# 14 of the 44 row tiles of a down projection, computed in 2x2 blocks with seven products instead of eight

## The chip, the cores and the metric

One core of a Trainium2 chip runs the whole program. The metric is the device time in microseconds, the median of three runs. Five engines have queues of their own: TensorE (PE, with PEld for its weight loads), VectorE (DVE), ScalarE (ACT), GpSimd (POOL) and SyncE (SP), which here only issues DMAs. Each queue is worked off in order.

## The reference, cut to what matters

One layer of a decoder trunk on 512 tokens with 2048 features. The part that changes is the gated feed-forward at its end:

```python
D_FF = 5632                                    # 44 tiles of 128
a, v = jnp.split(h @ w_up, 2, axis=-1)         # h: (512, 2048), w_up: (2048, 2 * D_FF)
conv = conv_b + sum(conv_w[t] * shifted(a, t) for t in range(3))
x = x + gate2 * ((jax.nn.silu(conv) * v) @ w_down)     # w_down: (D_FF, 2048)
return rms_norm(x, final_norm_g)
```

`gate2` is the last sixth of `silu(c) @ ada_w + ada_b`. All arithmetic has to keep float32 accuracy.

## The kernel before, in words

Features lie on partitions and the 512 tokens along the free dimension. For accuracy each operand of a matmul is split into a rounded high part and a low rest (fp32r, both 4 bytes), and a product is three matmuls: high x high, high x low, low x high (`mm3`, L147 to L149). Splitting takes one ACT instruction (a cast to the high part) and one DVE instruction (the subtraction): L118 and L119 for weights, L174 and L175 for activations.

**Up projection.** The first three of 44 tile pairs (gate and value) are plain matmuls with 512 columns. The other 41 ("groups", numbered from 0) are computed by a Strassen-Winograd scheme (`up_group`, `product`, `Fast`): the weights of a group are cut into 2x2 blocks (two halves of the features, and gate against value), the activations too (two halves of the features, two halves of the tokens), and seven products P1, Q5, P2, P7, Q3, P6, Q4, in this order, take the place of eight. A product ("step") is 8 feature tiles x 3 matmuls with 256 columns (L804 to L806); each product sums into one of four PSUM banks, and a few ACT and DVE instructions (L936 to L948) join them into the gate tile `a` and the value tile `v`.

`Fast` prepares the weights. Per group four DMAs of 512 KB on SP (L763) and two accumulating ones on POOL (L774) load blocks, two DVE additions form sums of blocks (L768 `first`, L778 `fourth`), and each of the seven weight operands is split (L118, L119). The event table puts each of these some steps ahead of its product. The pool `rp` for raw loads has nine buffers (two of them hold `ca`, the activated vector c, until the last modulation tile is done, and the weights of a running and of a coming group hold up to six), the pool `wp` for split weights has three, so the split for a step can begin when the product three steps back is done. The activations of the seven products (`hop`) are made once by `make_h` just ahead of group 0 and inside it: 28 splits of 128x512 and their sums.

At the end of a group the tile pair of the group before goes through `glu` (conv, silu, times v; L720 to L724) and is written to the DRAM tensor `ad` (L1010).

**Down projection.** It goes over the 44 tiles in chunks of `JD` = 10, 10, 10, 10 and 4. For each of 16 output tiles of a chunk, 10 weight tiles make 30 matmuls with 512 columns, and L1048 adds the result, times gate2 (`mods[5]`), to the residual `x1`, which is loaded back from DRAM in chunk 0 (L1019). The activations are read from `ad` two tiles at a time and split (`act_pair`, L989); for the first chunk this is done during the last up group (`drain`). The 16 tiles of gate2 are computed during chunk 0 (`ada_next`): two rows of 512 KB loaded (L94), multiplied with `ca` and summed on DVE (L100, twice a tile), and joined (L109). The last chunk of 4 runs in two halves of 256 tokens, with the final norm.

The order in each queue is not that of the code alone: a scheduler places instructions by its own estimates of when they are ready. The rows of the queues below are what it made.

Of the kernel before, what the change touches and what calls it, by code (L numbers as in the profile page):

```python
# [14 lines left out]
P = 128  # L15
# [6 lines left out]
JD = (10, 10, 10, 10, 4)  # L22
NDS = 16 * 40 // 8
# [13 lines left out]
def trunk_kernel(ctx: ExitStack, tc: tile.TileContext, x, c, ada, w_in, w_qft, pool_w, w_out, w_up, w_dn, cst, msk, out):  # L37
# [66 lines left out]
    def ada_tile(m, k):  # L104
        a = gemv(ada[m * KT + k], ca)
# [498 lines left out]
    adaq += [(m, k) for m in (2, 4, 3, 5) for k in range(KT)]  # L604
# [75 lines left out]
    while len(adaq) > 2 * KT:  # L680
        ada_next()
# [53 lines left out]
    class Fast:  # L735
# [55 lines left out]
    fast = Fast([[w_up[j, q] for q in range(4)] for j in range(NP0, NJ)])  # L791
    nstep = [0]

    def product(n, i, opnd, banks):
# [6 lines left out]
        for k in range(8):  # L801
# [4 lines left out]
            E.matmul(o, wL[:, sl], mH, start=False, stop=k == 7, skip_group_check=True)  # L806
# [80 lines left out]
    ad = dp.tile([NJ, P, T], F32, tag="ad", name="ad", bufs=1)  # L887

    def late(jj):
        for i in (2 * jj, 2 * jj + 1):  # L890
            V.tensor_scalar(raws[i], raws[i], biases[:, KT + i:KT + i + 1], None, ALU.add)
        nc.sync.dma_start(ad[jj], glu(jj, raws[2 * jj], raws[2 * jj + 1]))
# [12 lines left out]
    for jj in range(NP0):  # L905
# [16 lines left out]
    def up_group(n):  # L922
# [3 lines left out]
        for i in SEQ:  # L926
            if n == 0:
                while len(hop[i]) < 8:
                    next(mh, None)
            product(n, i, hop[i], b)  # L930
            if n == NJ - NP0 - 1:
                del hop[i]
                drain(i)
# [66 lines left out]
    def drain(i):  # L1000
        act_more(min(JD[0] // 2, i))
        if i >= P6:
            dn.load(2 * (i - P6) + 2)
            dn.split(i - P6 + 1)

    pend = None
    for n in range(NJ - NP0):
        r = up_group(n)
        if pend is not None:
            nc.sync.dma_start(ad[pend[0]], glu(*pend))  # L1010
        pend = r
    nc.sync.dma_start(ad[pend[0]], glu(*pend))

    x1 += [None] * KT
# [74 lines left out]
def _layout(inputs):  # L1089
# [70 lines left out]
```

## Time and profile before

| | |
|---|---|
| median of three runs | 2088.27 us (2086.49 to 2090.19) |
| profiled execution | 2086.56 us, span 2084.7 us |
| granted TensorE clock, mean | 0.995 |
| PE busy | 2048.5 us (98% of the span), 13010 matmuls |
| DVE busy | 1548.2 us (74%) |
| ACT busy | 925.0 us (44%) |
| DMA moved | 414.64 MB, 199 GB/s over the span |
| up projection in products | from 793 to 1587 us |
| down projection | from 1587 to 2070 us |

A busy PE says little, since matmuls overlap: the mean of one 256-column matmul reads 276 ns, while they start 113 ns apart. What counts is the number that start in a stretch, and the idle time that a wait puts in front of them.

### The profile page before, as it was taken

To read this page: it belongs to the slowest core of one execution; us is meant where nothing else is said; L and a number is where in the kernel's file an instruction comes from. 1 tells how busy PE (TensorE), PEld (TensorE's weight loads), DVE (VectorE), ACT (ScalarE), POOL (GpSimd) and SP (SyncE) were. 2 spreads that over 40 slices of the span, in tenths; PEclk is the share of its full clock that TensorE was granted. 3 is DMA by queue.
4 is the path that set the end of the run, shared out by engine and by line. 5 is a ranking of instruction groups with operands and counts; after the bars stand their busy time and mean duration, and the time that the engine had idled before them with its cause. 6 is when DMAs were issued, how large, how long until landed. Compare 5 with 4: busy or idle time off the path is not lost.

```text
span 2084.7 us, 32504 instructions
## 1 busy us (share of the span) xinstructions
PE 2048.5 (98%) x13010; PEld 1835.3 (88%) x13010; DVE 1548.2 (74%) x2311; ACT 925.0 (44%) x1330; POOL 94.1 (5%) x123
## 2 busy tenths in 40 slices
PE   7999999999999999999999999999999999999997
PEld 6888888888888888999999999999999888888887
DVE  8898899988977688887777777777778754343446
ACT  4323555565733355554544554455454222222234
POOL 0100000000000000000000000000000000000001
PEclk9999999999999999999999999999999999999998
DMA  9886877755586545787777777777778964343402
GB/s 372 314 295 211 280 236 251 247 174 181 192 301 220 195 170 124 205 229 177 179 185 180 173 187 183 177 174 191 182 176 301 323 240 142 102 134 102 139 30 81
DMA packets 127639, 414.64 MB, mean 199 GB/s; under 512 B 13536, under 2 KB 17920, under 8 KB 127488
## 3 DMA queue, kind: packets, MB, share of 16 engines
q1 hardware_dynamic: 115680, 369.57, 52.3%
q0 software_dynamic: 11808, 43.00, 12.5%
q8 instruction: 102, 1.67, 0.3%
q14 instruction: 49, 0.40, 0.1%
HBM read 392.58 MB, written 19.94 MB: 198 GB/s over the span
## 4 chain that ended last, share of the span: by engine, by line
PE 88%; DVE 6%; DMA 2%; issue 2%; ACT 1%; SPq 0%; DVEq 0%; POOL 0%; POOLq 0%; ACTq 0%
PE mm L147 11%; PE mm L149 11%; PE mm L148 11%; PE mm L806 7%; PE mm L804 7%; PE mm L805 7%; PE sm L805 5%; PE sm L806 5%; PE sm L804 5%; PE sm L148 4%; PE sm L147 4%; PE sm L149 4%; DMA raw<-in_dram 2%; DVE raw L100 1%; DVE w L119 1%
## 5 line engine op out<-in xcount | busy, mean ns | idle before, releaser
L118 ACT CAST w<-raw 128x1024 fp32r<-128x1024 f32 x491 | 516.3, 1052 | 766.2 <-PE mm L149 312.3
L119 DVE TENSOR_TENSOR w<-raw,w 128x1024 fp32r<-128x1024 f32 x491 | 600.3, 1223 | 323.4 <-ACT w L118 323.2
L147 PE MATMUL mm<-hh,w 128*128 128x512 f32 x1120 | 437.1, 396 | 14.9 <-ACT w L118 13.1
L149 PE MATMUL mm<-hh,w 128*128 128x512 f32 x1120 | 437.5, 391 | 0.0
L148 PE MATMUL mm<-hl,w 128*128 128x512 f32 x1120 | 436.6, 390 | 0.0
L806 PE MATMUL mm<-hh,w 128*128 128x256 f32 x1312 | 362.6, 276 | 0.7 <-DVE w L119 0.7
L805 PE MATMUL mm<-hl,w 128*128 128x256 f32 x1312 | 362.6, 276 | 0.3 <-DVE hl L175 0.2
L804 PE MATMUL mm<-hh,w 128*128 128x256 f32 x1312 | 362.5, 276 | 0.0
L100 DVE SCALAR_TENSOR_TENSOR raw<-raw,ca 128x1024 f32<-128x1024 f32 x192 | 232.1, 1219 | 74.9 <-DMA raw<-in_dram 74.1
L805 PE MATMUL sm<-hl,w 128*128 128x256 f32 x984 | 273.5, 278 | 4.5 <-DVE hl L175 4.5
L804 PE MATMUL sm<-hh,w 128*128 128x256 f32 x984 | 273.4, 278 | 0.0
L806 PE MATMUL sm<-hh,w 128*128 128x256 f32 x984 | 273.0, 277 | 0.0
L147 PEld LDWEIGHTS mm<-hh,w 128*128 128x128 f32 x1120 | 210.9, 188 | 59.1 <-ACT w L118 13.1
L149 PEld LDWEIGHTS mm<-hh,w 128*128 128x128 f32 x1120 | 210.7, 188 | 45.4 <-DVE w L119 0.8
L148 PEld LDWEIGHTS mm<-hl,w 128*128 128x128 f32 x1120 | 211.0, 188 | 42.6 <-issue 0.5
L806 PEld LDWEIGHTS mm<-hh,w 128*128 128x128 f32 x1312 | 246.3, 188 | 1.3 <-DVE w L119 1.1
L805 PEld LDWEIGHTS mm<-hl,w 128*128 128x128 f32 x1312 | 246.3, 188 | 0.7 <-DVE hl L175 0.7
L804 PEld LDWEIGHTS mm<-hh,w 128*128 128x128 f32 x1312 | 246.3, 188 | 0.4 <-ACT hh L174 0.4
L805 PEld LDWEIGHTS sm<-hl,w 128*128 128x128 f32 x984 | 186.0, 189 | 5.3 <-DVE hl L175 5.3
L804 PEld LDWEIGHTS sm<-hh,w 128*128 128x128 f32 x984 | 185.9, 189 | 0.5 <-ACT hh L174 0.2
L806 PEld LDWEIGHTS sm<-hh,w 128*128 128x128 f32 x984 | 186.1, 189 | 0.1
L148 PE MATMUL sm<-hl,w 128*128 128x512 f32 x384 | 149.4, 389 | 0.0
(198 smaller groups left out, 2532.6 us busy)
## 6 DMA issues: line engine op xcount, KB each, us to landing
raw<-in_dram SPq DMA_DIRECT2D x612, 512.0 KB, 4.8
raw<-in_dram POOLq DMA_DIRECT2D x82, 512.0 KB, 5.4
ad<-t SPq DMA_DIRECT2D x44, 256.0 KB, 3.1
raw<-ad SPq DMA_DIRECT2D x22, 512.0 KB, 3.8
t<-in_dram SPq DMA_DIRECT2D x32, 256.0 KB, 6.0
x1d<-t SPq DMA_DIRECT2D x16, 256.0 KB, 4.1
t<-x1d SPq DMA_DIRECT2D x16, 256.0 KB, 6.0
out_dram<-ob SPq DMA_DIRECT2D x8, 512.0 KB, 3.3
```

What stands on the lines that cost most here:

```text
L100: V.scalar_tensor_tensor(out=r, in0=r, scalar=1.0, in1=vec[i], op0=ALU.mult, op1=ALU.mult, accum_out=a[:, i:i + 1])
L118: A.copy(h, r)
L119: V.tensor_tensor(l, r, h.bitcast(F32), op=ALU.subtract)
L147: E.matmul(o, wH, mH, start=start, stop=False)
L148: E.matmul(o, wH, mL, start=False, stop=False)
L149: E.matmul(o, wL, mH, start=False, stop=stop)
L804: E.matmul(o, wH[:, sl], mH, start=first and k == 0, stop=False, skip_group_check=True)
L805: E.matmul(o, wH[:, sl], mL, start=False, stop=False, skip_group_check=True)
L806: E.matmul(o, wL[:, sl], mH, start=False, stop=k == 7, skip_group_check=True)
```

## The change

The first 14 tiles of the down projection are taken in 2x2 blocks with seven products, by the functions that the up projection has: 7 pairs of row tiles on one axis (even and odd tile), output tiles f and f + 8 on the other, and the two halves of the tokens. That gives 8 further groups (41 to 48) of seven products with 7 tiles x 3 matmuls with 256 columns each. The chunks behind them are `JD` = 10, 10, 6 and 4. In detail:

- `emit`: the results of `glu` for these 14 tiles are not written to `ad`. For each pair four DVE instructions of 128x256 form the sums that the products need, and four DMAs write seven blocks to a DRAM tensor `od`.
- `operands`, `handover`: during the last up group, behind each step, the activations of the same step of the down groups are read from `od` (two DMAs, 512 and 384 KB, in rows of 1 KB) and split: three splits of 128x512 and one of 128x256 per step, on ACT and DVE. Behind the steps of the last down group, the work of the old `drain` is done.
- `Fast` gets 8 more groups, with weight blocks of 128x896.
- The gate2 tiles (`mods[5]`) move from chunk 0 into the up groups 7, 9, ... 37, one in each.
- Both `x1` tiles of a down group are loaded at its head.

```diff
-JD = (10, 10, 10, 10, 4)
-NDS = 16 * 40 // 8
+SD = (7,)
+JD = (10, 10, 6, 4)
+NSP = sum(SD)
+NDS = 16 * sum(JD[:-1]) // 8
...
+        def new(self, n):
+            return rp.tile([P, U], F32, tag="raw", name="raw")[:, :self.groups[n][0].shape[-1]]
...
+    for m in SD:
+        for _ in range(8):
+            groups.append([])
+            for _ in range(4):
+                groups[-1].append(w_ds[off:off + P * m * P].rearrange("(p n) -> p n", p=P))
+                off += P * m * P
+    fast = Fast(groups)
...
-        for k in range(8):
+        for k in range(len(opnd)):
...
+    def emit(j, t):
+        if j >= 2 * NSP:
+            nc.sync.dma_start(ad[j - 2 * NSP], t)
+            return
+        held[j] = t
+        if j ^ 1 not in held:
+            return
+        p = j // 2
+        a, b = held.pop(2 * p), held.pop(2 * p + 1)
+        s, r = tt(), tt()
+        lo, hi = slice(0, 256), slice(256, 512)
+        V.tensor_tensor(s[:, lo], a[:, hi], b[:, hi], op=ALU.subtract)
+        V.tensor_tensor(s[:, hi], a[:, lo], a[:, hi], op=ALU.subtract)
+        V.tensor_tensor(r[:, hi], a[:, lo], s[:, lo], op=ALU.subtract)
+        V.tensor_tensor(r[:, lo], b[:, lo], r[:, hi], op=ALU.subtract)
+        for i, q in ((0, b), (2, s), (4, r)):
+            nc.sync.dma_start(od[i:i + 2, p].rearrange("i p t -> p i t"), q.rearrange("p (i t) -> p i t", i=2))
+        nc.sync.dma_start(od[6, p], a[:, lo])
...
+    def ada_load(k):
+        arow[k] = gemv_load(ada[5 * KT + k])
+
+    for k in range(KT):
+        todo[7 + 2 * k, P1] = partial(ada_load, k)
+        todo[7 + 2 * k, Q4] = partial(ada_tile, 5, k, arow)
...
+    def operands(c, i):
+        p0, m = sum(SD[:c]), SD[c]
+        res = []
+        for q in range(0, m, 4):
+            w = min(4, m - q)
+            r = rp.tile([P, U], F32, tag="raw", name="raw")
+            nc.sync.dma_start(r[:, :w * 256].rearrange("p (m t) -> p m t", m=w),
+                              od[OIX[i], p0 + q:p0 + q + w].rearrange("m p t -> p m t"))
+            for g in range(0, w, 2):
+                src = r[:, g * 256:(g + min(2, w - g)) * 256]
+                if w - g > 1:
+                    res += split2(src)
+                else:
+                    t = tp.tile([P, T], F32R, tag="t", name="hh")
+                    h, l = t[:, :256], t[:, 256:]
+                    A.copy(h, src)
+                    V.tensor_tensor(l, src, h.bitcast(F32), op=ALU.subtract)
+                    res.append((h, l))
+        return res
...
+    for n in range(NJ - NP0):
+        r = (n + NP0,) + group(n, hop, hop_ready if n == 0 else None, handover(0, hop) if n == NJ - NP0 - 1 else None)
+        if pend is not None:
+            emit(pend[0], glu(*pend))
+        pend = r
+    emit(pend[0], glu(*pend))
+    ng = NJ - NP0
+    for c in range(len(SD)):
+        for f in range(8):
+            if c == 0:
+                x1_load(f)
+                x1_load(f + 8)
+            a, v = group(ng, dop[c], None, handover(c + 1, dop[c]) if f == 7 else None)
+            ng += 1
+            for i, q in ((f + 8, v), (f, a)):
+                V.scalar_tensor_tensor(out=x1[i], in0=q, scalar=mods[5][:, i:i + 1], in1=x1[i], op0=ALU.mult, op1=ALU.add)
...
-            if ci == 0:
-                ada_next()
-                x1_load(f + 1)
```

The DVE queue in an up group of before, from the end of `glu` on. The three `w` rows ahead of L778 are the splits for P7, Q3 and P6, the one at the end is that for Q4; L768 and L778 are `first` and `fourth`:

```order
L724 TENSOR_TENSOR t_8480<-t_8480,t_8033 128x512
L119 TENSOR_TENSOR w_8527<-raw_8273,w_8527 128x1024
L768 TENSOR_TENSOR raw_8617<-raw_8500,raw_8498 128x1024
L119 TENSOR_TENSOR w_8555<-raw_8419,w_8555 128x1024
L119 TENSOR_TENSOR w_8583<-raw_8392,w_8583 128x1024
L778 TENSOR_TENSOR raw_8392<-raw_8392,raw_8362 128x1024
L942 TENSOR_TENSOR th_8494<-th_8494,mm_8488 128x256
L119 TENSOR_TENSOR w_8614<-raw_8392,w_8614 128x1024
```

The same stretch in group 9 of the change, one of the 16 groups with a gate2 tile:

```order
L726 TENSOR_TENSOR t_8971<-t_8971,t_8516 128x512
L102 SCALAR_TENSOR_TENSOR raw_9017,acc_9199<-raw_9017,ca_86 128x1024
L121 TENSOR_TENSOR w_9021<-raw_8764,w_9021 128x1024
L121 TENSOR_TENSOR w_9049<-raw_8910,w_9049 128x1024
L102 SCALAR_TENSOR_TENSOR raw_9018,acc_9199<-raw_9018,ca_87 128x1024
L773 TENSOR_TENSOR raw_9111<-raw_8990,raw_8988 128x1024
L121 TENSOR_TENSOR w_9077<-raw_8883,w_9077 128x1024
L983 TENSOR_TENSOR th_8984<-th_8984,mm_8978 128x256
L783 TENSOR_TENSOR raw_8883<-raw_8883,raw_8853 128x1024
L111 SCALAR_TENSOR_TENSOR mod5_102<-acc_9199,cs_78 128x1
L121 TENSOR_TENSOR w_9108<-raw_8883,w_9108 128x1024
```

The two L102 rows are new, and with the second of them L773 now stands between the splits for Q3 and P6.

SP in the last up group of before: the activations for chunk 0 (L989), then its weights (L965):

```order
L989 DMA raw_15975<-ad_6260 128x2x512
L989 DMA raw_16013<-ad_6260 128x2x512
L989 DMA raw_16052<-ad_6260 128x2x512
L1010 DMA ad_6260<-t_15905 128x512
L989 DMA raw_16090<-ad_6260 128x2x512
L989 DMA raw_16124<-ad_6260 128x2x512
L965 DMA raw_16134<-in_8_dram 128x1024
```

SP at the same place of the change, its first rows: L765 loads weights of group 41, L1056 the activations, of which there are 14:

```order
L765 DMA raw_16100<-in_8_dram 128x896
L765 DMA raw_16102<-in_8_dram 128x896
L1056 DMA raw_16129<-od_6253 128x4x256
L1056 DMA raw_16139<-od_6253 128x3x256
L1056 DMA raw_16176<-od_6253 128x4x256
L908 DMA ad_6252<-t_16082 128x512
L1056 DMA raw_16186<-od_6253 128x3x256
L1056 DMA raw_16223<-od_6253 128x4x256
L1056 DMA raw_16233<-od_6253 128x3x256
L765 DMA raw_16246<-in_8_dram 128x896
```

Five reads have become 14, and between them stand the weights of a further group.

The DVE queue of the change a little later, in group 41. The first two rows (L177, L1066) are the last activations for its last product Q4, `w_16602` and `w_16629` are the splits for P1 and Q5 of group 42, L723 to L726 are `glu` for the last two up groups, and L985 joins products:

```order
L177 TENSOR_TENSOR hl_16434<-raw_16431,hh_16433 128x512
L1066 TENSOR_TENSOR hh_16437<-raw_16431,hh_16437 128x256
L773 TENSOR_TENSOR raw_16576<-raw_16471,raw_16469 128x896
L723 SCALAR_TENSOR_TENSOR t_16440<-t_15868,cs_78,t_16440 128x511
L723 SCALAR_TENSOR_TENSOR t_16447<-t_16093,cs_78,t_16447 128x511
L724 SCALAR_TENSOR_TENSOR t_16440<-t_15868,cs_78,t_16440 128x510
L724 SCALAR_TENSOR_TENSOR t_16447<-t_16093,cs_78,t_16447 128x510
L121 TENSOR_TENSOR w_16602<-raw_16471,w_16602 128x896
L726 TENSOR_TENSOR t_16440<-t_16440,t_15869 128x512
L726 TENSOR_TENSOR t_16447<-t_16447,t_16094 128x512
L985 TENSOR_TENSOR th_16464<-th_16464,sm_16460 128x256
L121 TENSOR_TENSOR w_16629<-raw_16576,w_16629 128x896
```

None of these rows has a counterpart in before at this place, where chunk 0 follows; the first `glu` instructions now stand ahead of the split for P1 of group 42.

## Rows read from the trace of the kernel before

**Rows 1.** Page, part 4: the chain that ended last, by engine.
```profile
PE 88%; DVE 6%; DMA 2%; issue 2%; ACT 1%; SPq 0%; DVEq 0%; POOL 0%; POOLq 0%; ACTq 0%
```
**Rows 2.** Stretches: length, then busy us (instructions) of each engine, clock, DMA share, GB/s.
```profile
1000.00:1050.00 50.00, 50.00 (x444) 50.00 (x443) 37.44 (x42) 24.53 (x31) 4.32 (x5) 1.00 0.71 179
1600.00:1650.00 50.00, 50.00 (x222) 41.40 (x221) 36.75 (x58) 11.78 (x13) 0.00 (x0) 1.00 0.93 331
1700.00:1750.00 50.00, 50.00 (x223) 41.38 (x222) 20.72 (x24) 13.64 (x17) 0.00 (x0) 1.00 0.42 133
```
**Rows 3.** Timeline of PE: 168 matmuls of 256 columns apart, then 72 of 512.
```profile
936.66 0.28 PE L804 MATMUL mm<-hh,w 128*128 128x256 f32 x1
...
955.70 0.28 PE L804 MATMUL mm<-hh,w 128*128 128x256 f32 x1
...
1699.64 0.39 PE L147 MATMUL sm<-hh,w 128*128 128x512 f32 x1
...
1715.96 0.39 PE L147 MATMUL mm<-hh,w 128*128 128x512 f32 x1
```
**Rows 4.** Waits of PE: engine, tile, line, releaser: us, times, longest.
```profile
PE sm L805 <- DVE hl L175: 4.5, 2, 3.4
```
**Rows 5.** Timeline of DVE in one up group: start, us, instruction, idle before.
```profile
941.93 0.68 DVE L724 TENSOR_TENSOR t<-t 128x512 f32<-128x512 f32 x1
...
946.38 1.23 DVE L119 TENSOR_TENSOR w<-raw,w 128x1024 fp32r<-128x1024 f32 x1 [0.24 <-ACT w L118]
...
950.36 1.23 DVE L778 TENSOR_TENSOR raw<-raw 128x1024 f32<-128x1024 f32 x1
...
952.77 1.23 DVE L119 TENSOR_TENSOR w<-raw,w 128x1024 fp32r<-128x1024 f32 x1 [0.86 <-ACT w L118]
```
**Rows 6.** Page, part 5: groups of instructions: busy us, mean ns, idle before.
```profile
L100 DVE SCALAR_TENSOR_TENSOR raw<-raw,ca 128x1024 f32<-128x1024 f32 x192 | 232.1, 1219 | 74.9 <-DMA raw<-in_dram 74.1
```
**Rows 7.** Landing of DMAs: L763 in 900 to 1560, then L94 in 1580 to 1760.
```profile
DMA to landing us min/median/max: 3.2/4.5/10.8
...
DMA to landing us min/median/max: 4.4/5.9/7.1
```
**Rows 8.** Timeline of DVE in the last up group, where one follows on another.
```profile
1570.25 0.68 DVE L724 TENSOR_TENSOR t<-t 128x512 f32<-128x512 f32 x1
...
1580.90 0.41 DVE L942 TENSOR_TENSOR th<-th,mm 128x256 f32<-128x256 f32 x1
1581.23 0.68 DVE L175 TENSOR_TENSOR hl<-raw,hh 128x512 fp32r<-128x512 f32 x1
1581.83 1.22 DVE L119 TENSOR_TENSOR w<-raw,w 128x1024 fp32r<-128x1024 f32 x1
1582.97 0.68 DVE L175 TENSOR_TENSOR hl<-raw,hh 128x512 fp32r<-128x512 f32 x1
...
1590.18 0.74 DVE L722 SCALAR_TENSOR_TENSOR t<-t,cs 128x510 f32<-128x510 f32 x1
1590.84 0.74 DVE L721 SCALAR_TENSOR_TENSOR t<-t,cs 128x511 f32<-128x511 f32 x1
```
**Rows 9.** Timeline of PE in group 0, then stretches there as in rows 2.
```profile
808.84 0.58 PE L805 MATMUL sm<-hl,w 128*128 128x256 f32 x1 [3.42 <-DVE hl L175]
...
805.00:807.50 2.50, 0.41 (x4) 0.20 (x2) 2.50 (x4) 0.00 (x0) 0.00 (x0) 0.94 0.34 139
807.50:810.00 2.50, 1.17 (x5) 1.17 (x6) 2.50 (x5) 1.05 (x1) 0.00 (x0) 0.50 0.02 7
810.00:812.50 2.50, 1.88 (x9) 1.54 (x7) 2.50 (x4) 0.62 (x1) 0.00 (x0) 0.50 0.00 0
812.50:815.00 2.50, 2.02 (x7) 1.68 (x7) 2.50 (x4) 1.44 (x3) 0.04 (x1) 0.50 0.62 211
815.00:817.50 2.50, 2.50 (x11) 2.22 (x12) 1.87 (x4) 0.88 (x2) 0.83 (x1) 0.52 0.45 39
817.50:820.00 2.50, 2.27 (x17) 1.93 (x16) 2.08 (x3) 1.43 (x3) 0.00 (x0) 1.00 0.90 175
```

More of the change, by code (lines that the diff above doesn't have):

```diff
@@ L102, in gemv, with ada_tile @@
         return a
-    def ada_tile(m, k):
-        a = gemv(ada[m * KT + k], ca)
+    def ada_tile(m, k, rows=None):
+        a = gemv(ada[m * KT + k], ca, rows and rows.pop(k))
         if (m, k) == (1, 0):
@@ L603, in trunk_kernel @@
     del xs
-    adaq += [(m, k) for m in (2, 4, 3, 5) for k in range(KT)]
+    adaq += [(m, k) for m in (2, 4, 3) for k in range(KT)]
     bgen = bias_all()
@@ L679, in trunk_kernel @@
     hs = [split(ys.pop(k)) for k in range(NH)]
-    while len(adaq) > 2 * KT:
+    while len(adaq) > KT:
         ada_next()
@@ L780, in split @@
         def split(self, n, i, key, drop):
-            self.hl[n, i] = split_weights(self.raw[n, key], U, PLU[i])
+            self.hl[n, i] = split_weights(self.raw[n, key], self.groups[n][0].shape[-1], PLU[i])
             if drop:
@@ L789, in upto @@
             self.at = max(self.at, step)
-    fast = Fast([[w_up[j, q] for q in range(4)] for j in range(NP0, NJ)])
+    groups, off = [[w_up[j, q] for q in range(4)] for j in range(NP0, NJ)], 0
+    for m in SD:
[5 more added lines that the diff above has]
+    fast = Fast(groups)
     nstep = [0]
@@ L805, in product @@
             E.matmul(o, wH[:, sl], mL, start=False, stop=False, skip_group_check=True)
-            E.matmul(o, wL[:, sl], mH, start=False, stop=k == 7, skip_group_check=True)
+            E.matmul(o, wL[:, sl], mH, start=False, stop=k == len(opnd) - 1, skip_group_check=True)
     def new_banks():
@@ L891, in late @@
             V.tensor_scalar(raws[i], raws[i], biases[:, KT + i:KT + i + 1], None, ALU.add)
[L892 removed]
+        emit(jj, glu(jj, raws[2 * jj], raws[2 * jj + 1]))
         raws[2 * jj] = raws[2 * jj + 1] = None
@@ L911, in trunk_kernel @@
         if jj == 0:
-            while len(adaq) > KT:
+            while adaq:
                 ada_next()
@@ L926, in up_group @@
         for i in SEQ:
[L927 to L933, printed above, removed]
+            if ready is not None:
+                ready(i)
+            product(n, i, opnds[i], b)
             X, Y, Z, W = (b[k][:, :256] for k in "XYZW")
@@ L948, in up_group, with hop_ready @@
                 V.tensor_tensor(a[:, 256:], Z, u, op=ALU.add)
+            if done is not None:
+                done(i)
             if (n, i) in todo:
                 todo.pop((n, i))()
-        return n + NP0, a, v
+        return a, v
+    def hop_ready(i):
+        while len(hop[i]) < 8:
+            next(mh, None)
     seq = [(f, k) for ci, n in enumerate(JD) for f in range(KT) for k in range(n)]
@@ L998, in act_more, with handover, f @@
             npair[0] += 1
[L1000 to L1012, printed above, removed]
+    dop = []
+    def operands(c, i):
[17 more added lines that the diff above has]
+        return res
+    def handover(c, old):
+        def f(i):
+            old[i] = None
+            if c < len(SD):
+                dop[c][i] = operands(c, i)
+            else:
+                act_more(min(JD[0] // 2, i))
+                if i >= P6:
+                    if NDS:
+                        dn.load(2 * (i - P6) + 2)
+                        dn.split(i - P6 + 1)
+                    else:
+                        ws_next()
+        return f
+    for m in SD:
+        dop.append({})
     x1 += [None] * KT
```

27 lines of the change are left out of this document (18 added, 9 removed).

## The prediction, as it was put on record

> **What bounds the kernel now.** I read the chain that ended last first: 88% of it is PE [rows 1], so a change is worth what it takes from PE's issue or adds to its waits. The stretches come next. In the up groups 444 matmuls of 256 columns start in 50 us, in the down chunks 222 of 512, at a full clock and with no idle time [rows 2]. The pace is exact in the timeline: 168 matmuls of 256 columns take 19.04 us, 113.3 ns each; 72 of 512 take 16.32 us, 226.7 ns each [rows 3]. A column costs the same in both shapes, so a product saved is time saved, as long as PE is fed.
>
> What feeds it is DVE, busy 37.4 of 50 us in the up stage [rows 2]. That is where the views of waits matter. PE's largest wait inside the products is 4.5 us on the splits of the activations (L175) in group 0 [rows 4], the one place where a whole set of split activations is made while products run. The change builds a second such place.
>
> **The change, part by part.**
>
> *Matmuls.* Removed: 14 tiles x 16 output tiles x 3 = 672 matmuls of 512 columns, 672 x 226.7 ns = 152.3 us. Added: 8 groups x 7 products x 7 tiles x 3 = 1176 of 256 columns, 1176 x 113.3 = 133.3 us. Gain 19.0 us, all of it on the path. A down group lasts 147 x 113.3 = 16.7 us, a step of it 2.38 us.
>
> A rule speaks against it. The Trainium skill (TensorE: Matmul & The Clock Gate, "Back-to-back issue gap") gives each matmul a fixed 2.5 ns on top of its columns; 504 more matmuls would then take back 1.3 us, and the gain would be 17.7. The rows show 113.3 against 226.7 ns, a factor of two to the last digit, so no fixed part is seen here and the measurement decides.
>
> *Steady down groups.* DVE pitches, from rows that follow on each other without a gap [rows 8]: a 1024-column split or sum 1.14 us, 512 columns 0.60, 256 columns 0.33, a `glu` step 0.66. Between the points for 512 and 1024 I take 1.00 for 896. A down group then needs on DVE 9 x 1.00 + 5 x 0.33 + 2 x 0.66 (the x1 updates, taken like a `glu` step) = 12.0 of 16.7 us. An up group needs 9 x 1.14 + 5 x 0.33 + 2 x 0.66 + 0.60 = 13.8 of 19.04. The same share of 72%, and that one runs without a wait. Cost 0.
>
> *The sums for the pairs.* 7 pairs x 4 x 0.33 = 9.2 us on DVE, spread over groups 3 to 11, 1.3 us each beside 5 us of slack. In groups 3 to 5 two pairs and the late tiles come together; there I put 0.5 us. If nothing covered them it would be 9.2. The 28 extra DMAs are short and SP is mostly waiting.
>
> *The gate2 tiles.* In chunk 0 they cost PE nothing (50.00 of 50 us busy [rows 2]), so their leaving gains nothing. In the up groups they come into a chain with a limit. Each such group loads two rows. The nine raw buffers hold two of `ca`, six of weights and one row; the second row can only be loaded when DVE is through with the first. On the clock of one group of before [rows 5]: the first row's L100 can start when L724 is done, 942.6, and takes 1.22 us [rows 6], to 943.8. The second is then issued at about 943.9. DVE could take it when the split for Q3 is done, 946.38 + 1.14 = 947.5. Behind it in the queue stand L773, the split for P6, a joining, L783, and then the split for Q4: 947.5 + 1.2 + 1.14 + 1.14 + 0.33 puts the end of L783 (1.23 long) at 952.5; in before the split for Q4 starts 1.18 us after that end and lasts 1.23 [rows 5], so it ends at 954.9. PE wants it at 955.93 (third matmul of the product that starts at 955.70 [rows 3]). So the second row may land 1.0 us late, at 948.5, which is 4.6 us after its issue. Loads in the up stage land in 4.5 us at the median (3.2 to 10.8), gate2 rows in chunk 0 in 5.9 (4.4 to 7.1) [rows 7]. At 4.5 there is no wait; at 5.9 it is 1.3 us in each of 16 groups, 21 us. I take the row of the stage they move into, and for the later half of its landings 0.2 us a group: 3.2 us. Ends 0 and 21.
>
> *The new hand-over.* During group 40 and 41 DVE has, beyond its usual work, 7 steps x (3 x 0.60 + 0.33) = 14.9 us of new splits. Group 40 starts at 939.38 + 33 x 19.04 = 1567.7; `glu` of 38 leaves DVE free at 1570.85 [rows 8], 3.1 us in. From there to the last activation for Q4 of group 41 the queue holds 21 splits of 512 (12.6 us), 7 of 256 (2.3), 5 operations of 1024 (5.7), 9 of 896 (9.0) and 6 joinings (2.0): 31.6 us, end at 34.7. PE, unhindered, would start Q4 of 41 at 19.04 + 6 x 2.38 = 33.3 and group 42 at 35.7. Q4 then starts about 1 us late, when its own weights are split, and ends at 36.7. Behind it DVE has L773 (1.0), four `glu` steps (2.6) and only then the split for P1 of 42 (1.0): 39.3. Group 42 starts 3.6 us late, after PE has idled for some 2.6 us in one piece. Two more rounds of `glu` and the joinings make 0.2 and 1.0 us of waits at Q5 and P2, then DVE gains on PE. Without anything else 4.8 us.
>
> The clock adds to this. In group 0 PE waited from 805.4, the granted clock fell to half 1.8 us later (0.94 in the stretch to 807.5), and it came back at 817.4, 8.6 us after PE had resumed [rows 9]. I expect 2.6 us of idle time, more than those 1.8, so I take the fall to half, 1.2 of 2.4 GHz, as the likelier case. At half pace 8.6 us cost 4.3, and the later two waits vanish beneath them: 3.6 + 4.3 = 7.9, rounded 8.0. The nearest row says the same: from 805 to 820 only 53 of 132 matmuls started, 9.0 us lost. Ends: 0 (DVE orders it better than I add up) and 16 (DMA, below).
>
> *The second hand-over and the chunks.* It is `drain` of before, which ran without a wait, with two x1 updates more in a shorter group: 0, at most 3. The plain chunks keep their pace: 0.
>
> *Sum.* -19.0 + 0.5 + 3.2 + 8.0 = -7.3 us on the profiled execution's 2086.56, which is 2079.3. The median of the runs is 1.7 above that execution, so 2081.0.
>
> **The rivals.**
>
> *No fall of the clock, rows in time* (2074.7 us): -19.0 + 0.5 + 4.8 = -13.7 us. For it: the fall in group 0 came after thinner matmuls too, and my idle stretch is only 0.8 us longer than what preceded that fall; the median landing fits. Against it: each term is then at its kind end. If the scheduler's order also hides part of the 4.8, it goes to 2070.
>
> *The gate2 rows become the bound: slower* (2095 us). The place is the second L102 in groups 7 to 37, the price 1.3 us x 16 = 20.8 if the rows land as in chunk 0: -19.0 + 0.5 + 20.8 + 4.8 = +7.1. It decides from a wait of 0.6 us a group on, that is from a landing of 5.2 us. For it: one buffer for both rows, and an in-order queue in which weights stand behind them. Against it: in chunk 0 the DMA share was 0.93, in the up stage it is 0.71 [rows 2].
>
> *The transfers of the hand-over become the bound* (2088 us). 7 x 896 KB of activations, six blocks of 448 KB for group 41 and the rest of group 40 are some 10 MB in 32 us, 310 GB/s, where the busiest stretch here moved 331 at a share of 0.93 [rows 2]; the activations come in rows of 1 KB, through three or four free buffers. If each step's activations come 1 us later than DVE could take them, 7 to 8 us are added: -19.0 + 0.5 + 3.2 + 16 = +0.7.
>
> *The change does not do what it says.* The order shows 504 more matmuls, as counted; I give this nothing.
>
> **How the numbers follow.** Forecast 0.34, no fall of the clock 0.30, gate2 rows 0.17, transfers 0.13, and 0.06 for less of everything in between (2083 to 2086). About 0.2%, 4 us, is what a measurement of this kernel can tell from no change, so faster means under 2084.1 and slower over 2092.4. Faster: all of the first two cases and a third of the small one and of the transfers' lighter half, 0.68. Same: the rest of transfers and a light case of the gate2 rows, 0.17. Slower: 0.15. The range from 2071 to 2093 leaves out the best end of the second case and the upper half of the gate2 case; the forecast's own is 2077 to 2085.
>
> **What would show it.** Right: 113.3 ns between matmuls in groups 41 to 48; a wait of PE of 2 to 3 us at the first product of group 42, on L121, and a clock of 0.5 for some 10 us behind it; waits at Q4 of the 16 gate2 groups that sum to 0 to 6 us, with DVE waiting on the DMA of L96; none at the second hand-over. Wrong: waits at most of the 16 groups of over 0.6 us; activations that DVE waits for by DMA at the hand-over; or a PE that never falls back there, which would mean that my running sum on DVE is too long.

## The result, and the profile after

The change makes the kernel slower. Its median is 2099.44 us (2097.16 to 2101.43) against 2089.23 us (2086.49 to 2090.62) for the kernel before on the same chip, a ratio of 1.0055 with a 95% interval of 1.0043 to 1.0067. I had forecast 2081.0 us and faster. The profiled execution took 2100.28 us, with a span of 2098.5 us against 2084.7.

The chain that ended last, part 4 of the page, shows at once that PE is less alone on it than in [rows 1]. DMA, at 2% before, is now 10%:

```profile
PE 72%; DVE 12%; DMA 10%; issue 3%; ACT 3%; POOL 0%; DVEq 0%; SPq 0%; ACTq 0%; POOLq 0%
```

The stretches tell where, best by the matmuls that start in each (the first bracket). Here are those of the kernel before that [rows 2] do not hold, and then those of the change:

```profile
850.00:925.00 75.00, 74.51 (x654) 74.17 (x653) 64.96 (x85) 38.86 (x50) 6.91 (x8) 1.00 0.82 227
925.00:1550.00 625.00, 625.00 (x5517) 625.00 (x5516) 480.83 (x559) 312.35 (x394) 57.06 (x66) 1.00 0.72 181
```
```profile
850.00:925.00 75.00, 73.09 (x633) 72.14 (x632) 65.09 (x92) 37.23 (x48) 6.04 (x7) 1.00 0.82 228
925.00:1550.00 625.00, 618.17 (x5406) 615.28 (x5405) 509.02 (x647) 301.98 (x387) 57.07 (x66) 1.00 0.79 208
...
1600.00:1650.00 50.00, 44.31 (x357) 42.74 (x356) 43.12 (x64) 26.51 (x42) 6.04 (x7) 0.97 0.93 267
1650.00:1700.00 50.00, 47.41 (x405) 46.21 (x404) 33.19 (x42) 20.08 (x28) 4.35 (x5) 1.00 0.63 170
1700.00:1750.00 50.00, 48.13 (x418) 47.52 (x418) 37.34 (x50) 23.93 (x35) 3.45 (x4) 1.00 0.77 221
```

All matmuls here have 256 columns, 444 of them fill 50 us, and each one short is 113.3 ns lost. So 21 fewer in 850 to 925 are 2.4 us, 111 fewer in the up groups 12.6 us, 87 short in the hand-over 9.9 us, and 39 and 26 short in the down groups 7.4 us. Those 284 and 0.5 us ahead of 850 are 32.7 us given back, where the matmuls saved are worth 19.0. The timeline agrees: from the first to the last matmul of 256 columns it is 793.3 us before (793.28 to 1586.63) and 959.2 after (793.16 to 1752.32); the eight new groups should add 133.3 of the 165.9, so 32.6 are lost. Behind them, in the plain chunks, nothing is.

The list of PE's waits (engine, tile, line, releaser: us, times, longest) names only part of it, since it leaves out the shortest; the kernel before has none in these three stretches. First the up groups, then 1600 to 1650, then the down groups:

```profile
PE mm L818 <- DVE w L121: 6.6, 11, 0.9
```
```profile
PE mm L818 <- DVE w L121: 5.0, 4, 2.3
PE sm L818 <- DVE w L121: 0.6, 2, 0.4
```
```profile
PE mm L818 <- DVE w L121: 2.5, 4, 0.6
PE sm L818 <- DVE w L121: 1.9, 3, 0.6
```

Every one is on a split of weights on DVE (L121). What DVE and ACT waited for, further up the chain, differs in the three places.

**Up groups with a gate2 tile.** DVE around the wait of 0.66 us that PE has at 1191.78 (start, us, instruction, idle before):

```profile
1177.56 1.22 DVE L102 SCALAR_TENSOR_TENSOR raw<-raw,ca 128x1024 f32<-128x1024 f32 x1
...
1184.33 1.23 DVE L102 SCALAR_TENSOR_TENSOR raw<-raw,ca 128x1024 f32<-128x1024 f32 x1 [1.70 <-DMA raw<-in_dram]
...
1190.50 2.36 DVE L121 TENSOR_TENSOR w<-raw,w 128x1024 fp32r<-128x1024 f32 x2 [1.06 <-ACT w L120]
```

SP issues the second row at 1178.82, when the first L102 is through, and DVE can take it 5.5 us later. From there to the end of the split for Q4 (the first of the two in the last row) it is 7.4 us, the sum that I had made from [rows 5, 6]. By my sum the row was allowed to be 1.0 us late; it was 1.7, and this group took 0.9 us more than its 19.04. Over all 16 groups DVE waits 22.7 us for it, and in 14 of them the group is longer by that wait less 0.7 to 0.8 us. Group 15 has the same two L102, and the second waits so little that the group loses nothing:

```profile
1106.54 1.23 DVE L102 SCALAR_TENSOR_TENSOR raw<-raw,ca 128x1024 f32<-128x1024 f32 x1 [0.60 <-DMA raw<-in_dram]
```

So 10.7 of the 12.6 us lie in the 16 groups with a gate2 tile. Of the other 1.9, 1.2 lie in group 38, where `first` (L773) waits 2.05 us for a weight load.

**The hand-over.** PE's longest wait there, and what ACT did ahead of it:

```profile
1612.55 0.41 PE L818 MATMUL mm<-hh,w 128*128 128x256 f32 x1 [2.26 <-DVE w L121]
```
```profile
1608.31 0.94 ACT L120 CAST w<-raw 128x896 fp32r<-128x896 f32 x1 [3.23 <-DMA raw<-in_dram]
```

This is in group 41, not at the first product of group 42, where I looked for it. ACT stood before the cast for P7 of group 41 until the accumulating DMA for it had landed (issued on POOL at 1600.85), and the casts of activations that DVE needed queued behind that cast. From 1583 to 1650 ACT waits 7.2 us for loads of weights, and 0.5 us for the reads of `od`. Behind PE's wait the clock fell to half, 1.2 of 2.4 GHz, for a much shorter time than in [rows 9]:

```profile
1612.50:1615.00 2.50, 2.45 (x12) 2.45 (x13) 2.50 (x4) 1.43 (x3) 0.00 (x0) 0.56 1.04 375
1615.00:1617.50 2.50, 2.50 (x19) 2.50 (x19) 2.50 (x4) 1.38 (x4) 0.00 (x0) 0.76 0.89 325
1617.50:1620.00 2.50, 2.50 (x25) 2.50 (x24) 2.50 (x5) 2.25 (x4) 0.00 (x0) 1.00 0.88 265
```

At the first product of group 42, behind the two `glu`, PE waits 1.63 us more.

**The down groups.** Group 44 (the expectation of x1_behind below calls it 43) shows it: two waits of PE of 0.62 us, and ACT's cast for P6. The groups 44 to 46 are each some 2 us too long, group 47 1.0, group 43 0.5, and group 48 not at all.

```profile
1675.48 0.39 PE L818 MATMUL sm<-hh,w 128*128 128x256 f32 x1 [0.62 <-DVE w L121]
1678.78 0.39 PE L818 MATMUL mm<-hh,w 128*128 128x256 f32 x1 [0.62 <-DVE w L121]
```
```profile
1673.35 0.94 ACT L120 CAST w<-raw 128x896 fp32r<-128x896 f32 x1 [3.34 <-DMA raw<-in_dram]
```

The DMA is the accumulating one that turns the operand of Q5 into that of P6. It is issued when Q5 is split (1664.52) and lands 8.8 us later. The issues from 1665 to 1760 (tile, queue, times, KB, median us to landing):

```profile
raw<-in_dram SPq DMA_DIRECT2D x12, 448.0 KB, 5.6
raw<-in_dram POOLq DMA_DIRECT2D x8, 448.0 KB, 8.1
...
t<-x1d SPq DMA_DIRECT2D x8, 256.0 KB, 8.3
```

In the up groups, 925 to 1560, the same DMA with 512 KB lands in 5.7 us at the median. So 64 KB less take 2.4 us more.

### The profile page after: what moved, and what is told of

It is laid out like the page before. It is cut to its first block, busy times and chain, and to the rows that moved or that the text cites. A ratio compares the mean times of both kernels' runs of the same rounds, so it can differ in the third digit from the quotient of the medians.

```text
span 2098.5 us, 33876 instructions
## 1 busy us (share of the span) xinstructions
PE 2043.7 (97%) x13514; PEld 1849.7 (88%) x13514; DVE 1612.1 (77%) x2437; ACT 955.0 (46%) x1396; POOL 107.8 (5%) x139
## 4 chain that ended last, share of the span: by engine, by line
PE 72%; DVE 12%; DMA 10%; issue 3%; ACT 3%; POOL 0%; DVEq 0%; SPq 0%; ACTq 0%; POOLq 0%
PE mm L149 10%; PE mm L151 10%; PE mm L150 10%; DMA raw<-in_dram 9%; PE mm L818 6%; PE mm L816 6%; PE mm L817 6%; DVE w L121 4%; PE sm L816 4%; PE sm L817 4%; PE sm L818 4%; PE sm L149 3%; PE sm L150 3%; PE sm L151 3%; DVE raw L102 2%
## 5 line engine op out<-in xcount | busy, mean ns | idle before, releaser
L120 ACT CAST w<-raw 128x1024 fp32r<-128x1024 f32 (+1 forms) x519 | 535.7, 1039 | 742.2 <-PE mm L151 259.0
L121 DVE TENSOR_TENSOR w<-raw,w 128x1024 fp32r<-128x1024 f32 (+1 forms) x519 | 625.0, 1209 | 276.6 <-ACT w L120 275.9
L818 PE MATMUL mm<-hh,w 128*128 128x256 f32 x1536 | 429.2, 280 | 15.9 <-DVE w L121 15.7
L816 PE MATMUL mm<-hh,w 128*128 128x256 f32 x1536 | 426.9, 278 | 0.2 <-ACT w L120 0.2
L817 PE MATMUL mm<-hl,w 128*128 128x256 f32 x1504 | 417.7, 278 | 0.7 <-DVE hl L177 0.7
L149 PE MATMUL mm<-hh,w 128*128 128x512 f32 x1008 | 394.0, 398 | 14.2 <-ACT w L120 12.7
L151 PE MATMUL mm<-hh,w 128*128 128x512 f32 x1008 | 394.6, 392 | 0.0
L150 PE MATMUL mm<-hl,w 128*128 128x512 f32 x1008 | 393.6, 391 | 0.0
L818 PE MATMUL sm<-hh,w 128*128 128x256 f32 x1152 | 321.2, 279 | 3.1 <-DVE w L121 2.9
L816 PE MATMUL sm<-hh,w 128*128 128x256 f32 x1152 | 320.6, 278 | 0.1
L818 PEld LDWEIGHTS mm<-hh,w 128*128 128x128 f32 x1536 | 289.4, 188 | 21.0 <-DVE w L121 20.9
L816 PEld LDWEIGHTS mm<-hh,w 128*128 128x128 f32 x1536 | 289.2, 188 | 0.9 <-ACT w L120 0.4
L102 DVE SCALAR_TENSOR_TENSOR raw<-raw,ca 128x1024 f32<-128x1024 f32 x192 | 232.5, 1222 | 68.8 <-DMA raw<-in_dram 68.5
L149 PEld LDWEIGHTS mm<-hh,w 128*128 128x128 f32 x1008 | 190.0, 188 | 53.7 <-ACT w L120 12.7
L151 PEld LDWEIGHTS mm<-hh,w 128*128 128x128 f32 x1008 | 189.8, 188 | 40.7 <-DVE w L121 0.8
L818 PEld LDWEIGHTS sm<-hh,w 128*128 128x128 f32 x1152 | 217.6, 189 | 4.9 <-DVE w L121 4.7
L816 PEld LDWEIGHTS sm<-hh,w 128*128 128x128 f32 x1152 | 217.5, 189 | 0.8 <-ACT hh L176 0.5
L779 POOL DMA_DIRECT2D raw<-in_dram x98 | 84.9, 866 | 1213.4 <-DVE raw L773 444.4
```

Source lines behind the costliest of these rows:

```text
L102: V.scalar_tensor_tensor(out=r, in0=r, scalar=1.0, in1=vec[i], op0=ALU.mult, op1=ALU.mult, accum_out=a[:, i:i + 1])
L120: A.copy(h, r)
L121: V.tensor_tensor(l, r, h.bitcast(F32), op=ALU.subtract)
L149: E.matmul(o, wH, mH, start=start, stop=False)
L150: E.matmul(o, wH, mL, start=False, stop=False)
L151: E.matmul(o, wL, mH, start=False, stop=stop)
```

## The experiments

The table gives the ratio to the kernel before on the same chip, the time from the first to the last matmul of 256 columns (products), and the sums of PE's waits in four stretches, in us. Times and waits of the products are those of one traced execution each.

| kernel | ratio (95%) | products, us | 850-925 | 925-1550 | 1600-1650 | 1650-1740 |
|---|---|---|---|---|---|---|
| before | 1 | 793.3 | 0.5 | 0 | - | - |
| the change | 1.0055 (1.0043-1.0067) | 959.2 | 2.0 | 6.6 | 5.6 | 4.4 |
| ten_raw | 1.0015 (1.0006-1.0024) | 951.0 | 2.8 | 2.9 | 6.5 | 1.2 |
| gate2_spread | 1.0001 (0.9991-1.0010) | 946.5 | 2.0 | 0 | 4.2 | 3.9 |
| vector_sum | 1.0044 (1.0028-1.0060) | 953.9 | 2.4 | 6.5 | 5.4 | 0 |
| glu_later | 1.0045 (1.0029-1.0062) | 956.3 | 2.3 | 7.5 | 4.6 | 3.0 |
| x1_behind | 1.0038 (1.0024-1.0051) | 953.9 | 1.5 | 6.9 | 5.5 | 0.6 |
| no_reads | one run, 2090.91 us | 949.1 | 1.8 | 7.4 | 0 | 4.3 |
| no_pair_sums | one run, 2099.80 us | 960.6 | 0.8 | 9.9 | 6.2 | 3.7 |
| three_mends | 0.9967 (0.9955-0.9978) | 941.2 | 2.8 | 0 | 5.5 | 0 |
| three_mends_early | 0.9943 (0.9930-0.9957) | 937.0 | 1.5 | 0 | 3.7 | 0 |
| mends_p7 | 0.9944 (0.9931-0.9958) | 935.3 | 2.6 | 0 | 1.6 | 0 |
| rows_of_4096 | one run, 4163.68 us | - | - | - | - | - |
| rows_4096_again | one run, 2112.90 us | 969.7 | 2.1 | 7.7 | 7.1 | 6.1 |

Since the waits leave out the shortest, the second table gives what PE lost: how much longer the groups are, from first matmul to first matmul, than 168 matmuls (19.04 us) or 147 (16.66 us). Groups 39 and 40 together lose 0.5 us at most. (The edges differ from those of the stretches above, and with them the sums by some tenths.)

| kernel | 0 to 6 | 7 to 38 | 41 and 42 | 43 to 48 |
|---|---|---|---|---|
| before | 12.8 | 0 | - | - |
| the change | 15.8 | 12.6 | 9.7 | 7.3 |
| ten_raw | 15.4 | 8.1 | 10.9 | 2.8 |
| gate2_spread | 16.3 | 0 | 9.7 | 6.7 |
| vector_sum | 16.6 | 12.2 | 11.4 | 0 |
| glu_later | 16.4 | 13.2 | 6.6 | 6.3 |
| x1_behind | 14.6 | 13.5 | 11.0 | 1.0 |
| no_reads | 16.4 | 11.4 | 0 | 7.5 |
| no_pair_sums | 13.4 | 16.3 | 11.0 | 6.1 |
| three_mends | 17.3 | 0 | 9.5 | 0 |
| three_mends_early | 15.4 | 0 | 7.8 | 0.1 |
| mends_p7 | 16.5 | 0 | 4.1 | 0.3 |
| rows_4096_again | 15.9 | 12.5 | 13.8 | 13.7 |

Groups 0 to 6 vary by up to 2.7 us between kernels whose edits touch nothing there, so a difference of the products of 1 or 2 us says nothing by itself; the column of the stage says more.

**ten_raw**

```diff
-    tp = ctx.enter_context(tc.tile_pool(name="tp", bufs=73))
-    rp = ctx.enter_context(tc.tile_pool(name="rp", bufs=9))
+    tp = ctx.enter_context(tc.tile_pool(name="tp", bufs=71))
+    rp = ctx.enter_context(tc.tile_pool(name="rp", bufs=10))
```

> The changed kernel with ten raw buffers in place of nine, so that the second gate2 row of a group needs no longer wait until DVE is through with the first (paid for with two of the 73 activation tiles). Theory (the second row's buffer is the cause of the 10.8 us lost in groups 7 to 37): its waits fall below 3 us there, in all about 2091 us. Rival (the DVE work of two L102 in one group is the cause, not the wait for the load): the waits stay at 9 to 11 us, in all 2098 to 2100. Both theories leave the down groups as they are; a tenth buffer may take up to 2 us from the hand-over.

2090.43 us, the time that the theory gave, but its reason is only a part of it. What DVE waits for by DMA in the up groups, of the change and then of ten_raw:

```profile
DVE raw L102 <- DMA raw<-in_dram: 22.7, 16, 2.3
```
```profile
DVE raw L773 <- DMA raw<-in_dram: 34.7, 16, 3.8
```

The second row is never waited for any more. In the same 16 groups `first` (L773) now waits for a weight load, since the tenth buffer changed the order on SP and DVE. Group 9 shows both, on DVE, and then its whole length:

```profile
981.01 1.22 DVE L102 SCALAR_TENSOR_TENSOR raw<-raw,ca 128x1024 f32<-128x1024 f32 x1
...
982.16 1.22 DVE L102 SCALAR_TENSOR_TENSOR raw<-raw,ca 128x1024 f32<-128x1024 f32 x1
...
996.12 1.23 DVE L773 TENSOR_TENSOR raw<-raw 128x1024 f32<-128x1024 f32 x1 [2.11 <-DMA raw<-in_dram]
```
```profile
977.86:996.90 19.04, 19.04 (x170) 19.04 (x169) 15.09 (x19) 9.53 (x12) 1.73 (x2) 1.00 0.76 212
```

With two L102 right behind one another the group keeps its 19.04 us, as 15 of the 16 do. That answers the rival: in these groups DVE's work for a gate2 tile costs PE nothing. PE loses in the group that follows, behind the wait at L773: 5445 matmuls start in 925 to 1550, still 72 fewer than before, 8.2 us. The rest of the gain lies in the down groups (2.8 us lost in place of 7.3); why they gain is not shown.

**gate2_spread**

```diff
...
     for k in range(KT):
-        todo[7 + 2 * k, P1] = partial(ada_load, k)
-        todo[7 + 2 * k, Q4] = partial(ada_tile, 5, k, arow)
+        for i in range(2):
+            todo[7 + 2 * k + i, P1] = partial(row_load, k, i)
+            todo[7 + 2 * k + i, Q4] = partial(row_mul, k, i)
```

> The changed kernel with one gate2 row in each of the 32 groups 7 to 38, in place of two rows in every second group; nine raw buffers. Theory (wait for the second row's load): no group has a second row, the waits in groups 7 to 38 fall from 10.8 to under 2 us, in all 2090 us. Rival (DVE's load): the same work in twice the groups, half the excess in each; if the wait grows evenly with it, the sum stays near 10 us, in all 2098 to 2100; if there is slack below one row, it falls too, and ten_raw tells the two apart.

The two new functions, not shown, load and multiply one row each. 2088.63 us, level with the kernel before. The stretch of the up groups:

```profile
925.00:1550.00 625.00, 625.00 (x5515) 624.84 (x5514) 521.86 (x653) 312.83 (x395) 56.97 (x67) 1.00 0.81 212
```

DVE is busier than in the change (521.9 against 509.0 us), with the same 32 L102, and PE loses nothing. Alone this run cannot tell DVE's work from the wait, since it halves both in a group; with ten_raw and group 15 of the change it can. The cause is the second row, which has to wait for the buffer of the first. That one thing cost 12.6 us, more than the whole loss against the kernel before, 10.2 us.

**vector_sum**

```diff
-                self.put(s - 1, partial(self.dsum, n, "T", 3))
+                if n < NJ - NP0:
+                    self.put(s - 1, partial(self.dsum, n, "T", 3))
+                else:
+                    self.put(s + 1, partial(self.vsum, n))
...
+        def vsum(self, n):
+            t = self.raw[n, "T"]
+            V.tensor_tensor(t, t, self.raw[n, Q3], op=ALU.add)
```

> The changed kernel with the sum for P6 in the down groups (T plus the fourth block) made by one DVE addition of 128x896 from the block that Q3 uses, in place of the accumulating DMA on POOL. Theory (this DMA lands 7 us after its issue and holds the cast for P6, then all up to Q4): the two waits of 0.6 us a group in groups 42 to 48 go, 6.9 us falls to under 1.5, in all 2093 to 2094 us. Rival (DVE is too full in the short groups): 1.0 us more on DVE in each group, the waits stay or grow by up to 1 us a group, in all 2099 to 2107.

2095.67 us. Both at once: no wait is left behind 1650, and the hand-over is 1.7 us worse (second table). The additional addition of group 41 comes where DVE has no time: from 1612.65 to 1636.49 it works without a break. The clock falls there too (stretches as in [rows 2]):

```profile
1630.00:1635.00 5.00, 4.46 (x21) 4.16 (x21) 5.00 (x9) 0.50 (x1) 0.02 (x1) 0.50 0.94 213
...
1650.00:1700.00 50.00, 50.00 (x444) 50.00 (x443) 40.76 (x53) 22.26 (x30) 2.61 (x4) 1.00 0.61 166
```

444 matmuls in 50 us with blocks of 128x896: PE's pace in the down groups was forecast right, and DVE has time there even for one addition more; only the transfer was not foreseen.

**glu_later**

```diff
-        if pend is not None:
+        if pend is not None and n < NJ - NP0 - 1:
             emit(pend[0], glu(*pend))
...
+            if f >= 1 and ends:
+                q = ends.pop(0)
+                emit(q[0], glu(*q))
```

> The changed kernel with the last two glu moved behind groups 42 and 43. Theory (they stand ahead of the first split of group 42): the wait of 1.63 us at its first product goes and with it the 0.45 at the third, in all 2097 to 2098 us. Rival (the late loads for group 41 set the hand-over, and what is saved here is lost in the next wait): no change, 2099 to 2100; the work in groups 43 and 44 adds up to 1 us there.

2096.35 us, 2.9 us less in the products and 3.1 in groups 41 and 42: the wait of 1.63 us at the first product of group 42 is gone but for 0.26 us, and 1.14 and 0.63 us come back a little later in that group, where ACT's cast waits for the next accumulating DMA. The other long wait stays, 2.19 us at 1614.75, and here the clock does not fall behind it:

```profile
1612.50:1615.00 2.50, 0.31 (x3) 0.26 (x3) 2.50 (x6) 1.91 (x4) 0.00 (x0) 1.00 1.04 233
1615.00:1617.50 2.50, 2.50 (x23) 2.50 (x23) 2.50 (x4) 1.78 (x4) 0.00 (x0) 1.00 1.05 408
```

**no_reads**

```diff
...
-                dop[c][i] = operands(c, i)
+                dop[c][i] = keep[i][:6] + keep[i][:1]
```

> The changed kernel with the split activations of the up groups used again in the down groups: left out are the reads of od and the splits in groups 40 and 41. Theory (the hand-over's loss of some 9 us is the work and traffic of the new splits): waits of PE in 1600 to 1650 us fall from 5.6 to under 2, the clock does not fall, in all 2090 to 2092 us. Rival (the accumulating DMAs of the 128x896 blocks are late by themselves, as in groups 43 to 48): two waits of 0.6 us a group stay from group 41 on, and only 5 us go, 2094 us.

(`keep` holds the old activations.) The hand-over then costs nothing at all, in the stretch in which the change starts 357 matmuls:

```profile
1600.00:1650.00 50.00, 50.00 (x443) 50.00 (x442) 37.50 (x50) 24.00 (x34) 4.93 (x6) 1.00 0.74 199
```

The products are 10.0 us shorter, about the loss of that stretch. The waits of the down groups stay (4.3 us). Two causes, then, not one. The run takes out the new reads and the new splits together, so it does not tell which of the two the hand-over suffers from.

**rows_of_4096 and rows_4096_again**

```diff
-                groups[-1].append(w_ds[off:off + P * m * P].rearrange("(p n) -> p n", p=P))
-                off += P * m * P
+                groups[-1].append(w_ds[off:off + P * U].rearrange("(p n) -> p n", p=P))
+                off += P * U
...
```

> The changed kernel with the weight blocks of the down groups padded to 128x1024, so that their DMAs have rows of 4096 bytes in place of 3584; splits, sums and casts then go over 1024 columns too. Theory 1 (the row of 3584 bytes makes the accumulating DMA slow, 7.0 us at the median against 5.7): it lands in 5.4 to 5.9 us in groups 43 to 48. Theory 2 (what else runs on the queues at that moment sets it): 6.5 us or more, as in the change. In both the splits are 0.14 us longer, so waits of some 0.3 to 0.6 us at P6 and Q4 can stay; the time says less than the landing.

> The kernel of rows_of_4096 once more, since PE ran at half pace from end to end in that run, so that its groups lasted twice as long. Theory 1 (the row of 3584 bytes makes the accumulating DMA slow): it lands in 5.4 to 5.9 us at the median in groups 43 to 48. Theory 2 (the transfers that run beside it in the shorter groups do): 6.5 us or more, and waits of 0.6 us and more twice a group.

In the first of the two PE ran at half pace from end to end (span 4161.9 us; 216 matmuls of 256 columns start in 50 us in place of 444). Why is not known, and nothing else is read from it. In the second, from 1665 to 1770, the accumulating DMA with rows of 4096 bytes took:

```profile
raw<-in_dram POOLq DMA_DIRECT2D x9, 512.0 KB, 8.1
```

As long as with rows of 3584 bytes. The length of the row is not the cause. (The kernel is slower than the change, 2112.90 us in one run; its splits and sums are longer too.)

**x1_behind**

```diff
             if c == 0:
-                x1_load(f)
-                x1_load(f + 8)
+                todo[ng, Q3] = lambda f=f: (x1_load(f), x1_load(f + 8))
```

> The changed kernel with the two x1 tiles of a down group (512 KB) loaded in its middle; in SP's queue they then stand, from group 44 on, behind the two weight loads for the next group and no longer ahead of them. In the trace of the change all transfers of a group come in one burst (1663 to 1673.5 us in group 43: DMA share 1.0, then 0 until 1677), and the x1 loads were issued at 1662.55, between the two accumulating DMAs of 1661.62 and 1664.52. Theory (they share the engines with the accumulating DMA that ACT waits for): 512 KB less beside it at some 240 GB/s is 2 us; it lands in 5 to 6 us in groups 44 to 48, the waits of 0.6 us at P6 and Q4 there go, 4 to 5 us in all, 2094 to 2095.5 us. Rival (an accumulating DMA of a 128x896 block is slow by itself): it lands in 7 us as before, 2098 to 2100 us.

2094.99 us. That was most of it. The issues from 1665 to 1760, to be read against those of the change above, and the one wait of PE that is left in 1650 to 1760:

```profile
raw<-in_dram SPq DMA_DIRECT2D x12, 448.0 KB, 4.3
raw<-in_dram POOLq DMA_DIRECT2D x8, 448.0 KB, 6.6
...
t<-x1d SPq DMA_DIRECT2D x10, 256.0 KB, 5.0
```
```profile
PE mm L818 <- DVE w L121: 0.6, 1, 0.6
```

Two transfers of 256 KB, moved by a few places in a queue, are worth 6.3 of the 7.3 us that groups 43 to 48 lost. The accumulating DMA, 8.1 us beside them, lands in 6.6 without them, later than the 5 to 6 that I expected; the 0.9 us that it still takes longer than in the up groups are not explained by a run.

**no_pair_sums**

```diff
-        V.tensor_tensor(s[:, lo], a[:, hi], b[:, hi], op=ALU.subtract)
...
+        s, r = a, b
```

> The changed kernel with the four sums for each pair left out: od gets blocks of the same size straight from the results of glu. Theory (the sums stand in DVE's queue between late tiles and splits, and cost PE 1.3 us beyond what the stretch lost in the kernel before): waits of PE in 850 to 925 us fall from 2.0 to under 1.0, in all 2098 us. Rival (the sums are hidden, and the waits there are those of before, moved): 1.5 to 2.0 us of waits stay, 2099.4 us.

The waits of 850 to 925 fall to 0.8 us, and 651 matmuls start there, 18 more than in the change: 2.0 us, the cost of the sums. The time does not show it, since the waits of the gate2 groups rose to 9.9 us from 6.6; why they did is not shown.

**three_mends, three_mends_early, mends_p7.** gate2_spread, glu_later, and vector_sum from group 42 on; then also `first` of group 41 two steps earlier; then also the sum for P7 of group 42 on DVE. Only what they add to the edits above is shown:

```diff
-                self.put(s - 3, partial(self.first, n))
+                self.put(s - (5 if n == NJ - NP0 else 3), partial(self.first, n))
...
-            self.dsum(n, P7, 3)
+            if n == NJ - NP0 + 1:
+                self.put(7 * n + -1, partial(self.vsum, n, P7))
+            else:
+                self.dsum(n, P7, 3)
```

> Three edits together: one gate2 row in each of the groups 7 to 38; the sum for P6 by DVE in the down groups 42 to 48 (group 41 keeps the accumulating DMA, since DVE is full there); the last two glu behind groups 42 and 43. If the terms are separate, they add up: 11 us from gate2 (gate2_spread against the change), 6 from the waits of groups 43 to 48 (none are left in vector_sum behind 1650 us), 2 from glu, 2099.4 less 19 = 2080 us, 0.4% below the kernel before. Rival (what one mend gives comes back in the next wait, as the hand-over did in vector_sum): 2085 to 2090 us.

> The same with the first sum of blocks of group 41, and with it the accumulating DMA for its P7, put two steps earlier. Theory (that DMA, issued at 1600.85 and landed by 1608.3, held ACT's cast and all the splits behind it, and made the wait of 2.26 us in group 41): 2 us less than three_mends, 2078 us. Rival (DVE is full there in any case and the wait moves a few steps on): the same as three_mends.

> three_mends_early with the sum for P7 of group 42 made by DVE as well, in place of its accumulating DMA. Theory (that DMA, issued at 1608.97, held ACT's cast until 1618.50 and made the wait of 1.85 us of PE at 1619.49, behind which the clock was at half for some 3 us): that wait falls below 0.7 us and the clock does not fall there, 2074 to 2075 us against 2076.9. Rival (DVE is full in group 41 and 42, and the addition waits for the plain load of the same block): a wait of the same size remains, 2077 to 2078 us.

2081.51, 2076.92 and 2075.57 us. In three_mends the products are 18.0 us shorter than in the change, where the three parts one by one add up to 20.8; the waits of the hand-over stay at 5.5 us, so there the rival holds: what glu_later gave back by itself does not show in it. The earlier `first` takes 4.2 us more off the products. The 2 us that I expected are there, 2.3 us in groups 39 to 42; the other 2.0 lie in groups 0 to 6, which the edit does not touch. It moved the wait on, as the next accumulating DMA shows (POOL, ACT and PE of three_mends_early):

```profile
1608.97 0.86 POOL L782 DMA_DIRECT2D raw<-in_dram  x1 [13.91 <-DVE raw L776]
```
```profile
1618.50 0.94 ACT L120 CAST w<-raw 128x896 fp32r<-128x896 f32 x1 [5.22 <-DMA raw<-in_dram]
```
```profile
1619.49 0.38 PE L823 MATMUL mm<-hh,w 128*128 128x256 f32 x1 [1.85 <-ACT w L120]
```

In mends_p7 this wait is 0.39 us, and the clock holds:

```profile
1600.00:1650.00 50.00, 48.35 (x413) 47.27 (x413) 47.96 (x66) 26.79 (x41) 2.59 (x3) 1.00 0.77 231
```

Its products are 1.7 us shorter than those of three_mends_early; the two ratios cannot be told apart. Both are some 0.56% faster than the kernel before.

## Why the prediction was wrong

*The gain: right.* 19.0 us. Groups of 128x896 without waits keep 444 matmuls in 50 us (vector_sum), so the saved matmuls are saved time. In mends_p7 the products take 142.0 us more than before for eight groups that should take 133.3: 8.7 us of the 19.0 are still given back there, mostly in the hand-over and the sums.

*The gate2 tiles: the step that failed most.* "For the later half of its landings 0.2 us a group: 3.2 us" was 12.6 us. The mechanism was right to the line: second row, its wait, split for Q4. Its size was off. I had bounded the cost by a landing of 4.5 (nothing) and 5.9 us (1.3 a group), and chose the kind end, the median of a stage that had no such loads in it. With them in it, the weight loads of that stage land in 4.9 us at the median, and the second rows in 5.1 (4.3 to 6.0); 13 of the 16 are over the 4.6 us that I had allowed. My own rule with these landings gives 9.0 us, and the 16 groups lost 10.7. So the rule held, and the landing that I put into it was from the wrong loads. The rival that named it had 17 in 100; by its own sum and at the price measured it gives -19.0 + 0.5 + 12.6 + 4.8 = -1.1 us, no change. To be slower, the kernel needed the next term as well.

*The steady down groups: "Cost 0" was 7.4 us.* I compared DVE's share with that of the up groups, found the same 72%, and let that stand for the stage. The share was about right, 66% and 75% in the two stretches from 1650 to 1750. What I did not do is lay the group's transfers side by side: 16.7 in place of 19.0 us, and two x1 loads at its head that the up groups do not have. They ran between the accumulating DMAs, and ACT waited. The Trainium skill (DMA: Bandwidth & Descriptors, "Issuing engines are not separate DMA queues") says that DMAs of SP, ACT and POOL end up on the same engines and interleave. The runs agree: with SP's loads between them POOL's transfers took 8.1 us, and 6.6 without (x1_behind). The rule spoke against the change, and I did not weigh it.

*The hand-over: 8.0 forecast, 9.9 measured, by another way.* The wait behind the two `glu` came where I had put it, 1.63 us in place of 2.6. The longer one, 2.26 us, came a group earlier, from an accumulating DMA in the traffic of the hand-over and not from DVE's queue. The clock fell behind that one, for some 3 us and not 8.6. That the sum came close is luck. "Transfers of the hand-over become the bound" (by its own sum 2089.0 us, not 2088) was the better account of it, but it named the reads of activations, and ACT waited for weights.

*The pair sums: 0.5 forecast, 2.0 to 2.4 measured.* *Second hand-over and chunks: 0, right.*

In all 32.7 us were given back against 11.7 forecast. Of the difference of 21.0 us, 9.4 lie in the gate2 tiles and 7.4 in the steady down groups, and these two turned the sign; the hand-over and the sums add 1.9 us each. The common fault: I added up DVE's queue instruction by instruction, and took for a transfer a median from a stage with other neighbours, or no time at all.

## What to carry over

A share of busy time that stays the same says little of a shorter stage: write down, for one round of it, when each transfer is issued, what runs beside it, and when it is wanted. Where a load goes through a buffer that the same round has just freed, take its landing from loads that run beside the same transfers, and ask what the new loads do to that landing: here 5.1 in place of 4.5 us, in 16 groups, was most of that term's miss. And a change that brings back less than its matmuls promise may still hold all of it: here three small moves of loads and sums turned 0.55% slower into 0.33% faster, and two more made it 0.56%.

## What was not expected of the hardware

- The clock did not fall behind each wait of some 2 us. It did for 3 to 4 us behind 2.26 us in the change, 2.06 in three_mends and 1.85 in three_mends_early, and for some 7 us behind 2.09 in vector_sum; it did not behind 2.19 in glu_later. In group 0 it stays low for some 10 us [rows 9]. The length of a wait alone does not say what it costs.
- The landing of an accumulating DMA depends on its neighbours more than on its size: 5.7 us for 512 KB in the up groups, 8.1 us for 448 KB and for 512 KB alike beside the x1 loads, 6.6 us for 448 KB without them.
